# Loading x's first half and the first weight word in small transfers on two queues, in a two-layer encoder on one Trainium2 core

## The chip, the core and the metric

The kernel runs on one core of one Trainium2 chip. Its parts here are TensorE (PE: matrix products and the turning of 128x128 blocks; PEld is its weight load), VectorE (DVE), ScalarE (ACT), GpSimd (POOL) and SyncE (SP). Transfers from memory are issued by SP, ACT and POOL, each with a queue of its own (q1 is SP's, q10 is ACT's), and share 16 DMA engines. The metric is the device time of one execution in microseconds; before the change the median of three runs is 907.72 us (907.42 to 908.06).

## The reference

Two layers over x of 256 tokens by 1024 features, in float32. Each layer is: half a SwiGLU, a mixer (an mLSTM in layer 0, windowed attention in layer 1), half a second SwiGLU, each followed by a layer norm of `ALPHA * x + ...`:

```python
def swiglu(x, w_in, w_out):
    gu = x @ w_in
    g, u = gu[..., :D_FF], gu[..., D_FF:]
    return (jax.nn.silu(g) * u) @ w_out

def reference(x, ...):
    for l in range(DEPTH):
        x = layer_norm(ALPHA * x + 0.5 * swiglu(x, ffn_w_in[l, 0], ffn_w_out[l, 0]), ln_g[l, 0], ln_b[l, 0])
        j = l // N_MIXERS
        if l % N_MIXERS == 0:
            y = mlstm_mixer(x, ml_w_in[j], ml_gate_b[j], ml_norm_g[j], ml_w_out[j])
        else:
            y = window_attention(x, at_w_in[j], at_sink[j], at_w_out[j])
        x = layer_norm(ALPHA * x + y, ln_g[l, 1], ln_b[l, 1])
        x = layer_norm(ALPHA * x + 0.5 * swiglu(x, ffn_w_in[l, 1], ffn_w_out[l, 1]), ln_g[l, 2], ln_b[l, 2])
    return x
```

The change touches only what happens ahead of and during the first products of the first SwiGLU, `x @ w_in`.

## The kernel before

**Products.** Every float32 operand is split in two parts of a shorter format, high (`_hi`) and low (`_lo`), and each product is made of three: high x high, low x high and high x low. For x the split needs x turned: TensorE turns 128x128 blocks of x with the identity matrix `ident` (rows `py<-ident,x`), one engine casts the turned block to `xT_hi` and DVE subtracts to get `xT_lo`. x lies in two tiles of 128 tokens (`x_72`, `x_73` in the instruction lists), each loaded in two halves of 512 features. The products read `xT` as the stationary operand and a word of weights as the moving one.

**Words.** Weights come in words of 128 partitions by 1024 numbers (512 KB). A word lands in `w_raw` (four buffers, and one further one later) or `s_raw` (words that are also summed with others); ACT casts it to `w_hi`, DVE subtracts to get `w_lo`. Only word 0 is cast and subtracted in two halves of 512 numbers (one for each 128 rows of the weight matrix), so that its first products can start after the first half.

**The opening.** ACT issues the four loads of x (tile 0 half 0, tile 1 half 0, tile 0 half 1, tile 1 half 1), then loads its activation table. SP issues the words: as many as there are buffers, then each further one when a buffer comes free. `ident` is made on POOL and DVE. In `ffn`, at the very start, TensorE runs `warm(14)`, 14 idle turns of `ident` into a bank that nobody reads; then turns tile 0's half 0, whose cast is DVE's; then `warm(8)`. The function `first_mm` then writes out the order of the first two words: for word 0 the high x high pair for tile 0, the turns of tile 1's half 0 (cast by ACT), the x-low pair, the w-low pair, and the three pairs for tile 1; for word 1 first the turns of both second halves (eight turns), then the pairs.

**What sets the order elsewhere.** TensorE's order is the program's. The casts, subtractions and sums of words are placed by a planner (`Paced` and `Weights.fill`): it keeps a model of each engine's time and of when each load lands (`moving`, with constants for issuing, landing and loading), and after each product decides which cast, subtraction or sum fits next; a freed buffer then lets SP issue the next word. So a change in the modelled time of the opening can change the order of later words on ACT, DVE and SP. Each engine runs its own list strictly in order.

## Time and profile before

| | |
|---|---|
| median of three runs | 907.72 us (907.42 to 908.06) |
| profiled execution, first to last instruction (span) | 906.0 us |
| around the span (median less span) | 1.7 us |
| TensorE busy | 896.5 us, 4419 products and turns |
| DVE, ACT, POOL busy | 799.4, 568.9, 142.0 us |
| x's first quarter lands | 5.39 us after the span's start |
| first product | 6.93 us |

The page gives the profiled execution's time as its span; the runs' times are 1.7 us above it, and the same is taken for both kernels. How to read the rows quoted below: a timeline row has the start in us, the length in us, engine, line, operation, written tile <- read tiles, shape, count, and in brackets how long the engine had been idle and what ended that. A row of the waits has who waited, for whom, us in total, times, the longest. A row of the windows has the window, its length, the busy time of PE, PEld, DVE, ACT and POOL with instruction counts, the granted TensorE clock, the DMA share and GB/s. A tile's row has an engine, operation and tiles, a count, and the shortest, median and longest length in ns with the first and last start. A queue's row has the packets so far, MB, and the share of the 16 engines. L179 is the line of the helper that records every operation, so rows are told apart by their tiles.

### The profile page before, as it was taken

Reading aid. Unit: us, or ns where it says so; the run is one execution under the profiler, and the core shown is the slowest. Engines: PE = TensorE matmul, PEld = TensorE weight load, DVE = VectorE, ACT = ScalarE, POOL = GpSimd, SP = SyncE. Lnnn points to the kernel's source line nnn. Section 1 sums busy time; section 2 is a strip of 40 time slices with the busy share of each in tenths; the row PEclk is TensorE's granted clock in tenths of the full one; section 3 lists DMA queues with packets and bytes.
Section 4 is the critical chain, followed back from the end, with each engine's and each line's share of the span. In section 5 each row is a group of like instructions: output and inputs, shape, how many; then the busy total and the mean of one; then the engine's idle time right before and its main releaser. Section 6 shows DMA issues by size and latency. Waiting matters only on the chain.

```text
span 906.0 us, 12445 instructions
## 1 busy us (share of the span) xinstructions
PE 896.5 (99%) x4419; PEld 748.8 (83%) x4419; DVE 799.4 (88%) x971; ACT 568.9 (63%) x782; POOL 142.0 (16%) x177
## 2 busy tenths in 40 slices
PE   9999999999999999999999999999999999999996
PEld 7888888889988888888888888888897788888885
DVE  5999899877799898999988899998867899899985
ACT  5776777356664666766636676765568566676760
POOL 0111123112211011211011112110414111111110
PEclk9999999999999999999999999999999999999999
DMA  8999998545637888998868989987333788899851
GB/s 278 367 321 274 256 301 218 171 141 182 214 99 248 306 233 238 290 274 247 235 202 280 241 265 275 286 203 238 122 111 117 246 267 257 207 302 267 243 140 47
DMA packets 100734, 208.54 MB, mean 230 GB/s; under 512 B 6920, under 2 KB 21296, under 8 KB 100672
## 3 DMA queue, kind: packets, MB, share of 16 engines
q1 hardware_dynamic: 82368, 173.04, 54.7%
q0 software_dynamic: 17728, 33.66, 22.1%
q10 hardware_dynamic: 576, 1.05, 0.3%
q8 instruction: 35, 0.57, 0.2%
q14 instruction: 27, 0.22, 0.1%
HBM read 206.65 MB, written 1.05 MB: 229 GB/s over the span
## 4 chain that ended last, share of the span: by engine, by line
PE 98%; DVE 1%; DMA 1%; issue 0%; DVEq 0%
PE pw L179 63%; PE py L179 35%; DMA x<-in_x_dram 1%; DVE x L179 0%; DVE w_lo L179 0%; DVE stats L179 0%; DVE pr L179 0%; DVEq L1622 0%; DVE q_lo L179 0%; DVE mv L179 0%; DVE rs L179 0%
## 5 line engine op out<-in xcount | busy, mean ns | idle before, releaser
L179 DVE TENSOR_TENSOR w_lo<-w_raw,w_hi 128x1024 fp32r<-128x1024 f32 (+1 forms) x213 | 255.0, 1217 | 24.9 <-ACT w_hi L179 23.2
L179 ACT CAST w_hi<-w_raw 128x1024 fp32r<-128x1024 f32 (+1 forms) x213 | 218.8, 1049 | 73.2 <-PE py L179 18.8
L179 DVE TENSOR_TENSOR w_lo<-s_raw,w_hi 128x1024 fp32r<-128x1024 f32 x192 | 228.3, 1217 | 18.0 <-ACT w_hi L179 18.0
L179 ACT CAST w_hi<-s_raw 128x1024 fp32r<-128x1024 f32 x192 | 196.4, 1054 | 59.8 <-DVE s_raw L179 30.4
L179 PE MATMUL pw<-w_hi,xT_hi 128*128 128x512 f32 x480 | 156.1, 395 | 0.0
L179 PE MATMUL pw<-w_hi,xT_lo 128*128 128x512 f32 x480 | 153.5, 390 | 0.0
L179 PE MATMUL pw<-w_lo,xT_hi 128*128 128x512 f32 x480 | 153.4, 390 | 0.0
L120 POOL DMA_DIRECT2D s_raw<-in_ffn_w_in_dram x64 | 77.4, 1210 | 482.6 <-DVE s_raw L179 253.5
L179 PE MATMUL py<-w_hi,h_hi 128*128 128x512 f32 x349 | 117.3, 396 | 0.0
L179 PE MATMUL py<-w_hi,h_lo 128*128 128x512 f32 x349 | 115.5, 390 | 0.0
L179 PEld LDWEIGHTS pw<-w_lo,xT_hi 128*128 128x128 f32 x480 | 90.1, 188 | 19.0 <-DVE w_lo L179 0.3
L179 PEld LDWEIGHTS pw<-w_hi,xT_lo 128*128 128x128 f32 x480 | 90.0, 188 | 19.0
L179 PE MATMUL py<-w_lo,h_hi 128*128 128x512 f32 x349 | 104.8, 390 | 0.0
L179 PEld LDWEIGHTS pw<-w_hi,xT_hi 128*128 128x128 f32 x480 | 88.1, 188 | 16.5 <-ACT w_hi L179 0.2
L179 PE MATMUL pw<-w_hi,S_lo 128*128 128x512 f32 x256 | 78.8, 389 | 0.0
L179 PE MATMUL pw<-w_hi,S_hi 128*128 128x512 f32 x256 | 78.8, 389 | 0.0
L179 PE MATMUL pw<-w_lo,S_hi 128*128 128x512 f32 x256 | 78.8, 389 | 0.0
L179 PEld LDWEIGHTS py<-w_hi,h_lo 128*128 128x128 f32 x349 | 65.5, 188 | 14.4 <-DVE h_lo L179 0.4
L179 DVE TENSOR_TENSOR s_raw<-s_raw,s_raw 128x1024 f32<-128x1024 f32 x64 | 76.7, 1218 | 0.3
L179 PEld LDWEIGHTS py<-w_lo,h_hi 128*128 128x128 f32 x349 | 65.6, 188 | 13.4
L179 PEld LDWEIGHTS py<-w_hi,h_hi 128*128 128x128 f32 x349 | 64.7, 188 | 12.6 <-DVE S L179 0.2
L179 PEld LDWEIGHTS pw<-w_hi,S_lo 128*128 128x128 f32 x256 | 48.1, 188 | 10.0
(201 smaller groups left out, 1084.4 us busy)
## 6 DMA issues: line engine op xcount, KB each, us to landing
s_raw<-in_ffn_w_in_dram SPq DMA_DIRECT2D x96, 512.0 KB, 8.0
w_raw<-in_ffn_w_out_dram SPq DMA_DIRECT2D x88, 512.0 KB, 6.6
w_raw<-in_ffn_w_in_dram SPq DMA_DIRECT2D x64, 512.0 KB, 6.3
s_raw<-in_ffn_w_in_dram POOLq DMA_DIRECT2D x64, 512.0 KB, 8.3
w_raw<-in_ml_w_in_dram SPq DMA_DIRECT2D x24, 512.0 KB, 4.6
w_raw<-in_ffn_w_in_dram SPq DMA_DIRECT2D x32, 256.0 KB, 5.7
w_raw<-in_at_w_in_dram SPq DMA_DIRECT2D x12, 512.0 KB, 4.6
w_raw<-in_ml_w_out_dram SPq DMA_DIRECT2D x8, 512.0 KB, 3.9
```

The source lines that it names most:

```text
L120: self.nc.gpsimd.dma_start(ap, source, accum_op=OP.add)
L179: r = f(out, *args, **kw)
```

## The change

A new function `load_both` issues one load as two, rows 0 to 63 on SP's queue and rows 64 to 127 on ACT's, and tells the planner's model of it once. The two first halves of x (both tiles) go through it in place of one load on ACT's queue each. Word 0 goes through it twice, once for each half of 512 numbers. The second halves of x stay on ACT's queue, every other word on SP's. The idle turns ahead of the first products go from 14 to 10 and from 8 to 6.

```diff
+    def load_both(self, ap, source):
+
+        for r, engine in ((slice(0, 64), self.nc.sync), (slice(64, 128), self.nc.scalar)):
+            engine.dma_start(ap[r], source[r])
+        self.moving(0, ap, LANDING, LOADING * int(np.prod(ap.shape[1:])) / 1024, ISSUING)
+
...
-            nc.load(t.rearrange("p (k f) -> p k f", k=self.words[i]["k"]), self.words[i]["src"])
+            to = t.rearrange("p (k f) -> p k f", k=self.words[i]["k"])
+            if i == 0:
+                for k in range(self.words[i]["k"]):
+                    nc.load_both(to[:, k], self.words[i]["src"][:, k])
+            else:
+                nc.load(to, self.words[i]["src"])
...
-        nc.load(xt[t][:, s_], x[0, t * 128:(t + 1) * 128, s_], nc.nc.scalar)
+        if h == 0:
+            nc.load_both(xt[t][:, s_], x[0, t * 128:(t + 1) * 128, s_])
+        else:
+            nc.load(xt[t][:, s_], x[0, t * 128:(t + 1) * 128, s_], nc.nc.scalar)
...
-                warm(14)
+                warm(10)
                 to_xT(0, xt[0], ybank, (0,), nc.vector.tensor_copy)
                 W.split(1)
-                warm(8)
+                warm(6)
```

ACT, from its first instruction, before (DMA is the issue of a load; `x_72` and `x_73` are the two token tiles, `w_raw` a word):

```order
L111 DMA x_72<-in_x_dram 128x512
L111 DMA x_73<-in_x_dram 128x512
L111 DMA x_72<-in_x_dram 128x512
L111 DMA x_73<-in_x_dram 128x512
L593 ACT_TABLE_LOAD
L179 CAST w_hi<-w_raw 128x512 x2
L179 CAST xT_hi<-py 128x4x128
```

and with the change:

```order
L122 DMA x_72<-in_x_dram 64x512
L122 DMA w_raw<-in_ffn_w_in_dram 64x512 x2
L122 DMA x_73<-in_x_dram 64x512
L111 DMA x_72<-in_x_dram 128x512
L111 DMA x_73<-in_x_dram 128x512
L607 ACT_TABLE_LOAD
L185 CAST w_hi<-w_raw 128x512 x2
L185 CAST xT_hi<-py 128x4x128
```

Six issues stand ahead of the table load and the first cast in place of four, and the second halves of x come fifth and sixth in place of third and fourth.

SP, from its first instruction, before (an `s_raw` is a word that is also summed, `L114` a word in two strips):

```order
L116 DMA w_raw<-in_ffn_w_in_dram 128x2x512 x8
L116 DMA s_raw_211<-in_ffn_w_in_dram 128x2x512
L114 DMA w_raw<-in_ffn_w_in_dram 128x2x256 x2
L116 DMA s_raw_222<-in_ffn_w_in_dram 128x2x512
L114 DMA w_raw<-in_ffn_w_in_dram 128x2x256 x4
L116 DMA s_raw_257<-in_ffn_w_in_dram 128x2x512
```

and with the change:

```order
L122 DMA x_72<-in_x_dram 64x512
L122 DMA w_raw<-in_ffn_w_in_dram 64x512 x2
L122 DMA x_73<-in_x_dram 64x512
L116 DMA w_raw<-in_ffn_w_in_dram 128x2x512 x7
L116 DMA s_raw_210<-in_ffn_w_in_dram 128x2x512
L114 DMA w_raw<-in_ffn_w_in_dram 128x2x256 x2
L116 DMA s_raw_225<-in_ffn_w_in_dram 128x2x512
L114 DMA w_raw<-in_ffn_w_in_dram 128x2x256 x2
L116 DMA s_raw_240<-in_ffn_w_in_dram 128x2x512
```

Word 1 is now SP's fifth issue in place of its second, and further on a summed word goes ahead of a strip word.

DVE, ahead of the third down product (between the first two turns of `hh` of 256 columns and the `h_lo` of 512), before:

```order
L179 TENSOR_TENSOR hh_487<-sg_485,pw_380 128x256
L179 TENSOR_TENSOR w_lo_499<-w_raw_359,w_hi_449 128x1024
L179 TENSOR_TENSOR w_lo_512<-w_raw_387,w_hi_475 128x1024
L179 TENSOR_TENSOR w_lo_523<-s_raw0_211,w_hi_505 128x1024
L179 TENSOR_TENSOR w_lo_534<-s_raw0_257,w_hi_516 128x1024
L179 TENSOR_TENSOR s_raw0_211<-s_raw0_211,s_raw2_361 128x1024
L179 TENSOR_TENSOR s_raw0_257<-s_raw0_257,s_raw2_389 128x1024
L179 TENSOR_TENSOR w_lo_559<-w_raw_423,w_hi_527 128x1024
```

and with the change:

```order
L185 TENSOR_TENSOR hh_484<-sg_482,pw_373 128x256
L185 TENSOR_TENSOR w_lo_496<-w_raw_346,w_hi_448 128x1024
L185 TENSOR_TENSOR s_raw0_210<-s_raw0_210,s_raw2_384 128x1024
L185 TENSOR_TENSOR w_lo_515<-s_raw0_240,w_hi_475 128x1024
L185 TENSOR_TENSOR w_lo_526<-s_raw1_225,w_hi_502 128x1024
L185 TENSOR_TENSOR s_raw0_240<-s_raw0_240,s_raw2_394 128x1024
L185 TENSOR_TENSOR w_lo_543<-w_raw_400,w_hi_519 128x1024
L185 TENSOR_TENSOR w_lo_555<-w_raw_406,w_hi_530 128x1024
```

The word that TensorE uses last ahead of the third down product (`w_lo_499` before, `w_lo_543` with the change) moves from the first place behind `hh` to the sixth. The lists of all engines are the same again from about the place that the trace before reaches at 60 us, and TensorE's list differs only in the two counts of idle turns.

## The prediction

> **What bounds the kernel now.** I read the page's busy times and chain first, then the waits of TensorE.
>
> ```profile
> PE 896.5 (99%) x4419; PEld 748.8 (83%) x4419; DVE 799.4 (88%) x971; ACT 568.9 (63%) x782; POOL 142.0 (16%) x177
> PE 98%; DVE 1%; DMA 1%; issue 0%; DVEq 0%
> PE py L179 <- DVE ident L179: 1.7, 1, 1.7
> PE py L179 <- DMA x<-in_x_dram: 0.4, 1, 0.4
> ```
>
> TensorE (PE) is busy for 896.5 of 906.0 us and carries 98% of the chain. In the whole execution it has two recorded waits, 1.7 us for the identity matrix and 0.4 us for x, both at the start. So the change has only the opening to win. Here are the windows and, merged in order of time, the opening itself (start, length, engine, work):
>
> ```profile
> 0.00:7.00 7.00, 4.85 (x27) 4.25 (x27) 1.10 (x3) 2.42 (x3) 0.47 (x6) 1.00 0.69 236
> 7.00:12.00 5.00, 5.00 (x27) 3.88 (x28) 3.89 (x6) 2.41 (x4) 0.00 (x0) 1.00 1.05 388
> 40.00:60.00 20.00, 20.00 (x92) 16.55 (x91) 20.00 (x21) 13.49 (x17) 3.62 (x3) 1.00 1.07 322
> 0.79 2.54 ACTq L111 DMA_DIRECT2D x<-in_x_dram  x4
> 1.72 3.25 PE L179 MATMUL py<-ident 128*128 128x128 f32 x14 [1.72 <-DVE ident L179]
> 3.37 1.28 ACT L593 ACT_TABLE_LOAD   x1 [3.37 <-issue]
> 5.39 0.66 PE L179 MATMUL py<-ident,x 128*128 128x128 f32 x4 [0.43 <-DMA x<-in_x_dram]
> 5.72 1.14 ACT L179 CAST w_hi<-w_raw 128x512 fp32r<-128x512 f32 x2 [1.07 <-DMA w_raw<-in_ffn_w_in_dram]
> 6.09 0.69 DVE L179 CAST xT_hi<-py 128x512 fp32r<-128x512 f32 x1 [4.43 <-PE py L179]
> 6.82 0.69 DVE L179 TENSOR_TENSOR xT_lo<-py,xT_hi 128x512 fp32r<-128x512 f32 x1
> 6.93 0.70 PE L179 MATMUL pw<-w_hi,xT_hi 128*128 128x512 f32 x2
> 7.42 1.28 DVE L179 TENSOR_TENSOR w_lo<-w_raw,w_hi 128x512 fp32r<-128x512 f32 x2
> 7.50 0.42 PEld L179 LDWEIGHTS py<-ident,x 128*128 128x128 f32 x4 [0.31 <-DMA x<-in_x_dram]
> 7.92 0.70 PE L179 MATMUL pw<-w_hi,xT_lo 128*128 128x512 f32 x2
> 8.20 0.59 ACT L179 CAST xT_hi<-py 128x512 fp32r<-128x512 f32 x1 [1.34 <-PE py L179]
> 8.46 0.80 PE L179 MATMUL pw<-w_lo,xT_hi 128*128 128x512 f32 x2
> 8.76 0.19 PEld L179 LDWEIGHTS pw<-w_lo,xT_hi 128*128 128x128 f32 x1 [0.34 <-DVE w_lo L179]
> 9.10 0.62 PE L179 MATMUL pw<-w_hi,xT_hi 128*128 128x512 f32 x2
> 9.56 0.63 PE L179 MATMUL pw<-w_lo,xT_hi 128*128 128x512 f32 x2
> 10.48 1.03 PE L179 MATMUL py<-ident,x 128*128 128x128 f32 x8
> 11.27 0.71 PE L179 MATMUL pw<-w_hi,xT_hi 128*128 128x512 f32 x2
> ```
>
> The reader is to see two branches that meet at 6.93. In one, x's first quarter lands (5.39), is turned by TensorE, and is cast by DVE (6.09 to 6.78). In the other, the first word of weights lands and ACT casts its halves from 5.72 to 6.86. Behind 6.93 a pair of products starts 0.46 us after the one before (9.10, 9.56), four turns take 0.41 (7.51 to 7.92) and eight 0.79 (10.48 to 11.27). From 6.93 to 11.27 lie six pairs, four turns and eight: 6 x 0.46 + 0.41 + 0.79 = 3.96 of 4.34 us. The other 0.38 us is short waits, mostly for x (7.50) and for w_lo (8.76). Behind 11.27 TensorE waits for nothing in either window, so what is gained or lost by then passes to the end unchanged. I use 11.27, the first pair behind the eight turns, as the mark.
>
> **The change, part by part.** Durations of the issues, and how many packets each queue had moved by 3.5 us (first two queue rows) and 4.5 us:
>
> ```profile
> L111 ACTq DMA_DIRECT2D x<-in_x_dram x4: 453/489/1027, 0.8 to 2.3; - x4
> DMA to landing us min/median/max: 4.6/6.8/8.2
> q1 hardware_dynamic: 82, 0.17, 28.4%
> q10 hardware_dynamic: 32, 0.07, 4.9%
> q1 hardware_dynamic: 194, 0.40, 35.3%
> q10 hardware_dynamic: 127, 0.25, 14.2%
> ```
>
> *x's first quarter* (q10 is ACT's queue). It is 128 packets of 2 KB; 127 packets of q10 had started by 4.5 and the landing was seen at 5.39, so landing follows by 0.9 us. By 3.5 us both queues together had started 114 packets, but most of them were weights. With x at the head of both queues its 128 packets are out between 3.6 (all share evenly) and 3.85 (ACT's queue, the slower one, needs 64: between its 32 at 3.5 and 127 at 4.5). Plus 0.9 that is 4.5 to 4.75; I take 4.65, 0.74 earlier. The turns, DVE's cast (0.70 behind the turns' start, as 5.39 to 6.09) and the product (0.15 behind the cast's end of 6.78) move along: the x branch allows the first product at 6.93 - 0.74 = 6.2.
>
> *The first word.* Its first half is packets 129 to 256, and 321 had started by 4.5: about 4.25 + 0.9 = 5.15. But ACT now issues six transfers before its table load, not four. Three of the four took some 0.48 us, the last 1.03. The next two cost 0.45 to 1.03 each, and if the long one goes with larger transfers, all six may take 0.45. So the table load starts between 0.79 + 6 x 0.46 = 3.6 and 0.79 + 3 x 0.48 + 3 x 1.03 = 5.3, and ends 1.28 later, at 4.9 to 6.6. I take one long issue and five short: 0.79 + 5 x 0.48 + 1.03 = 4.2, end 5.5. Casts then run 5.55 to 6.69 in place of 5.72 to 6.86: the word's branch gains only 0.17. Cover that hid four issues (they ended at 3.33, the word came at 5.72) is used up by six.
>
> *The sum.* First product 6.2; the second needs the second cast half, 6.69 + 0.07 = 6.76. The turns of x's second row block follow at 6.76 + 0.23 = 6.99 (its data is behind 512 packets, about 5.4 + 0.9 = 6.3, so the wait at 7.50 is gone). Then come xT_lo's pair at 7.40 and w_lo's at 7.86; DVE, 0.74 earlier than at 7.42 to 8.70, makes w_lo from 6.68 to 7.96, in time for both products. The next pair needs ACT's cast of the turned block, 0.69 + 0.59 behind the turns' start, as 7.51 to 8.20 to 8.79: 8.27, so 8.35. It and two more pairs end at 9.73, the eight turns at 10.52: the mark comes 0.75 earlier. The last x block now leaves ACT behind five other transfers. It landed at 2.3 + 8.2 = 10.5, and its turns want it at 9.73 + 0.4 = 10.13. If it lands as before, the mark is 10.5 + 0.41 = 10.91, a gain of 0.36. With half of x's first blocks moved to SP's queue it should come somewhat earlier. Between 0.36 and 0.75 I take **0.6 us**.
>
> *Idle turns.* Eight of 22 go. They cost nothing where they wait for x anyway; the first ten end well before 4.65. What they cover is the clock:
>
> ```profile
> L179 PE MATMUL py<-ident x14: 421/421/476, 1.7 to 4.5; 128*128 128x128 f32 x14
> L179 PE MATMUL py<-ident x8: 272/272/273, 5.9 to 6.7; 128*128 128x128 f32 x8
> ```
>
> The first 14 take 421 ns each and start 0.215 us apart, the later ones 272 ns. So TensorE was at a lower speed until after 4.5 and at full speed by 5.39, though the windows' clock column shows 1.00 throughout. Ten turns end near 4.0, and a gap of 0.6 us follows. This could delay the step; it is a rival below, and costs nothing in the forecast.
>
> The Trainium skill ("TensorE: Matmul & The Clock Gate", section "The HAM clock gate (the "warmup" mystery)") says that the clock doubles after a free-running window of about 3.4 us of sustained work. The trace agrees in kind: 3.25 us of turns, then the faster ones. By that rule a window with ten turns and a gap in it may not count, which speaks against this edit; an estimate from the page's 3.4 us puts the step at 4.65 + 3.4 = 8.05 then, where the rows give 7.9 (rival 1).
>
> *The order behind it.* The planner now takes other words first, on ACT, DVE and SP, up to about 60 us; TensorE's order stays. From 40 to 60 us DVE is busy 20.00 of 20.00, so a word pushed back there could come late. The one pushed back most is the second weight word ahead of the third down product (w_lo_499 before, w_lo_543 now).
>
> ```profile
> 43.43 2.35 DVE L179 TENSOR_TENSOR w_lo<-w_raw,w_hi 128x1024 fp32r<-128x1024 f32 x2
> 53.15 0.61 PE L179 MATMUL pw<-w_lo,xT_hi 128*128 128x512 f32 x2
> ```
>
> It was started at 43.43 and used at 53.15. Five steps of its length (2.35 / 2 = 1.18 us) now stand ahead of it: start 49.3, ready 50.5. TensorE wants it 2.6 us later, 2.0 us if TensorE is 0.6 early and DVE is not. I cost this at nothing.
>
> **Rivals.** 1. *The clock comes later (slower).* It decides if the step to full speed waits for another unbroken 3.25 us of work. From the restart at 4.65 that is 7.9. Until then turns start 0.215 apart and pairs, at the same ratio, some 0.9. Four turns 4.65 to 5.5, six idle ones to 6.8, the first pair to 7.7, four turns to 8.2 (one slow, three fast), five pairs to 10.5, eight turns: the mark at 11.3, no change, **907.7**. So 7.9 is the point from which it decides: each us that the step comes later costs 0.5. If a stretch is broken again, the next ends at 11.15; halfway, 9.5, costs 0.8: **908.5**, and 11.15 costs 1.6: 909.3. For it: ten turns and a gap. Against it: only 0.6 us is missing, and turns of x fill in.
>
> 2. *The table load is late.* At its upper bound the casts run 6.6 to 7.74, the second product at 7.81, 1.05 behind the forecast's: 0.6 becomes -0.4, **908.1**; halfway, no change. For it: the fourth issue's 1.03 us. Against: half as many rows in each transfer.
>
> 3. *The transfers do not do what they are for.* Smaller ones start no sooner: q1 and q10 moved 114 packets by 3.5 us, whoever owned them. With x at 5.2 only 0.2 is won: **907.5**.
>
> 4. *A word comes late* at 50 to 53 us, if DVE slips by over 2.0 us, say because one of the sums ahead of it has to wait for its transfer. A slip of 3 us would cost 1.0 and leave **908.1**. For it: DVE is full there. Against: TensorE's two recorded waits are both at the start, so such margins have held everywhere.
>
> **Numbers.** The median is 907.72, 1.7 us above the profiled span of 906.0; I take that rest as fixed. Forecast: 907.72 - 0.6 = **907.1**, chance 0.53 (own range 906.7 to 907.5). Clock 0.17 (half of it beyond 7.9), table load 0.15, no earlier landing 0.10, late word 0.05. With the upper bound of the gain (casts at 5.2, from the word's landing: first two products unbroken, 0.33 more and about 1.0 in all, 906.7), the slower rivals at 908.1 to 908.5 and some 0.3 of scatter below (the runs shown span 0.64), I give 906.3 to 908.5. A measurement of this kernel can tell about 0.2%, 1.8 us. The gain cannot reach that: with x at 4.5 at the earliest and 1.54 from its landing to the first product (5.39 to 6.93) it is 0.9 there, and 0.38 of waits behind it, 1.3 in all. Only a clock that misses its second stretch, or a late word on top of another loss, comes near it on the other side. So faster 0.04, same 0.91, slower 0.05.
>
> **What would show it.** The first turns of x at 4.65 (right if 4.4 to 4.9); ACT's table load starting at 4.2 and the first cast at 5.55; the pair behind the eight turns at 10.5 to 10.9 in place of 11.27; the turns of x 272 ns long at once, where 421 would mean rival 1; and no new wait of TensorE between 12 and 60 us. The prediction is wrong if that mark does not move, or if the span changes by more than the mark.

## The result: 2.1 us slower, and the profile after

The changed kernel takes **910.17 us** in the median of ten runs (908.83 to 913.10) against 908.10 us for ten runs of the kernel before beside them: ratio 1.0028, 95% interval 1.0020 to 1.0036. A second measurement (further down) gives 1.0039, 1.0026 to 1.0053. The forecast was 907.1 us, in a range of 906.3 to 908.5, with a chance of 0.05 for slower. It was wrong in sign. Two of the runs further down, one of 1093 us (word 0 in whole rows) and one of 1295 us (first quarter only), had a granted clock of 0.78 and 0.65 in place of 0.99 or more and are left out of every comparison.

The profiled execution has a span of 908.2 us against 906.0. From the page of the changed kernel, busy time:

```profile
PE 898.0 (99%) x4413; PEld 750.0 (83%) x4413; DVE 799.7 (88%) x971; ACT 568.3 (63%) x782; POOL 142.1 (16%) x177
```

TensorE is busy 1.5 us longer with six turns fewer (4413 in place of 4419 instructions): it has not more to do, it does it more slowly. The opening of the changed kernel, in order of time (L185 is the helper, before it was L179; columns as in the prediction's rows):

```profile
0.80 0.57 ACTq L122 DMA_DIRECT2D x<-in_x_dram  x1
1.40 1.26 ACTq L122 DMA_DIRECT2D w_raw<-in_ffn_w_in_dram  x2
2.68 0.62 ACTq L122 DMA_DIRECT2D x<-in_x_dram  x1
3.55 1.45 ACTq L111 DMA_DIRECT2D x<-in_x_dram  x2
...
4.21 1.09 PE L185 MATMUL py<-ident,x 128*128 128x128 f32 x4
5.03 1.28 ACT L607 ACT_TABLE_LOAD   x1 [5.03 <-DMA w_raw<-in_ffn_w_in_dram]
5.08 1.49 PE L185 MATMUL py<-ident 128*128 128x128 f32 x6
6.32 1.14 ACT L185 CAST w_hi<-w_raw 128x512 fp32r<-128x512 f32 x2
6.99 1.31 PE L185 MATMUL pw<-w_hi,xT_hi 128*128 128x512 f32 x2 [0.42 <-ACT w_hi L185]
8.30 1.08 PE L185 MATMUL py<-ident,x 128*128 128x128 f32 x4
9.04 1.20 PE L185 MATMUL pw<-w_hi,xT_lo 128*128 128x512 f32 x2
10.04 0.96 PE L185 MATMUL pw<-w_lo,xT_hi 128*128 128x512 f32 x2
10.83 0.62 PE L185 MATMUL pw<-w_hi,xT_hi 128*128 128x512 f32 x2
12.21 1.03 PE L185 MATMUL py<-ident,x 128*128 128x128 f32 x8
13.01 0.70 PE L185 MATMUL pw<-w_hi,xT_hi 128*128 128x512 f32 x2
```

The first turns of x start at 4.21, earlier than forecast. But the first product is at 6.99 (before 6.93), and the mark, the pair behind the eight turns, is at 13.01 in place of 11.27: 1.74 us later. The first product waits for the first cast, and in this profile the cast waits for ACT's table load, which ends at 6.31. The word's first half was there before. The first row gives the landings of its two loads (issued at 1.40 and 1.44), the second those of x's second block (issued at 2.68 and 2.98):

```profile
DMA to landing us min/median/max: 3.2/3.7/4.1
DMA to landing us min/median/max: 4.9/5.1/5.2
```

So the word's first half had landed by 5.5, and x's second block landed at 8.2. Three things are new, then: the first product is held by the table load; the turns of x's second block start at 8.30 in place of 7.51; and everything up to the pair at 10.04 runs slowly (four turns 1.08 and 1.09 us, a pair 1.31 and 1.20), as the rows of the turns, for the first 12 us, show:

```profile
L185 PE MATMUL py<-ident x16: 417/417/473, 1.7 to 6.2; 128*128 128x128 f32 x16
L185 PE MATMUL py<-ident,x x8: 417/421/446, 4.2 to 9.0; 128*128 128x128 f32 x8
```

No turn up to 9.0 us takes the 272 ns that the eight idle turns took before; TensorE reaches full speed only ahead of the pair at 10.83 (0.62 long). The 1.74 us split so: the second block late, 8.30 less 7.51 = 0.79; its turns 0.74 us up to the next pair in place of 0.41, +0.33; that pair 1.00 up to the next in place of 0.54, +0.46; the next 0.79 in place of 0.64, +0.15; from there both kernels take the same (2.18 and 2.17). So 0.94 is the slow clock. The 0.79 has two causes that overlap: the block landed at 8.2, and the slow pair ahead of it would by itself have held the turns until about 8.0 (an estimate: its second product starts at 7.58, and later slow products follow each other by 0.43).

TensorE's waits in the whole execution:

```profile
PE py L185 <- DVE ident L185: 1.7, 1, 1.7
PE pw L185 <- ACT w_hi L185: 0.4, 1, 0.4
PE py L185 <- DVE S L185: 0.3, 1, 0.3
```

The wait for x is gone from the list and one for w_hi has come: the word's cast now comes last. (The wait ahead of 8.30 does not appear: the row before it is drawn up to 8.30, and the idle time of the weight load is put down to "issue".) The third wait, at 503 us, adds some 0.4 us to the shift; it is treated with the run on the order.

What the queues moved between 3 and 8 us, before and then after (the last column is GB/s):

```profile
3.00:8.00 5.00, 4.57 (x29) 3.65 (x27) 1.88 (x3) 2.42 (x3) 0.00 (x0) 1.00 1.01 383
```

```profile
3.00:8.00 5.00, 4.48 (x18) 3.27 (x16) 2.41 (x4) 2.42 (x3) 0.00 (x0) 1.00 0.91 234
```

The DMA engines are nearly as busy (0.91 against 1.01) and deliver 234 in place of 383 GB/s. The prediction counted packets at the pace of the kernel before. Up to 5.5 us that pace held (524 packets of both queues against 537), but 98 of them were small ones under 512 B in place of 32. From 5.5 to 8 us only 296 packets started in place of 532.

### The profile page after: what moved, and what is told of

It is laid out like the page before. It is cut to its first block, busy times and chain, and to the rows that moved or that the text cites. A ratio compares the mean times of both kernels' runs of the same rounds, so it can differ in the third digit from the quotient of the medians.

```text
span 908.2 us, 12436 instructions
## 1 busy us (share of the span) xinstructions
PE 898.0 (99%) x4413; PEld 750.0 (83%) x4413; DVE 799.7 (88%) x971; ACT 568.3 (63%) x782; POOL 142.1 (16%) x177
## 3 DMA queue, kind: packets, MB, share of 16 engines
q10 hardware_dynamic: 608, 1.05, 0.4%
HBM read 206.65 MB, written 1.05 MB: 229 GB/s over the span
## 4 chain that ended last, share of the span: by engine, by line
PE 95%; DVE 2%; DMA 1%; ACT 0%; issue 0%; ACTq 0%; DVEq 0%
PE pw L185 60%; PE py L185 35%; DMA w_raw<-in_ffn_w_out_dram 1%; DVE w_lo L185 1%; DMA w_raw<-in_ffn_w_in_dram 0%; DVE x L185 0%; DVE s_raw L185 0%; DVE S L185 0%; ACT w_hi L185 0%; DVE stats L185 0%; DVE S_lo L185 0%; ACT L607 0%; DVE pr L185 0%; DVEq L1636 0%; DVE q_lo L185 0%
## 5 line engine op out<-in xcount | busy, mean ns | idle before, releaser
L185 DVE TENSOR_TENSOR w_lo<-w_raw,w_hi 128x1024 fp32r<-128x1024 f32 (+1 forms) x213 | 255.1, 1219 | 26.4 <-ACT w_hi L185 25.2
L185 ACT CAST w_hi<-w_raw 128x1024 fp32r<-128x1024 f32 (+1 forms) x213 | 218.4, 1050 | 70.9 <-PE py L185 20.9
L185 DVE TENSOR_TENSOR w_lo<-s_raw,w_hi 128x1024 fp32r<-128x1024 f32 x192 | 228.6, 1219 | 17.9 <-ACT w_hi L185 17.8
L185 ACT CAST w_hi<-s_raw 128x1024 fp32r<-128x1024 f32 x192 | 196.5, 1054 | 61.0 <-DVE s_raw L185 31.7
L185 PE MATMUL pw<-w_hi,xT_hi 128*128 128x512 f32 x480 | 156.6, 397 | 0.4 <-ACT w_hi L185 0.4
L185 PE MATMUL pw<-w_hi,xT_lo 128*128 128x512 f32 x480 | 154.0, 391 | 0.0
L185 PE MATMUL pw<-w_lo,xT_hi 128*128 128x512 f32 x480 | 153.6, 391 | 0.0
L185 PE MATMUL py<-w_hi,h_hi 128*128 128x512 f32 x349 | 117.5, 396 | 0.3 <-DVE S L185 0.3
L185 PE MATMUL py<-w_hi,h_lo 128*128 128x512 f32 x349 | 115.3, 390 | 0.0
L185 PEld LDWEIGHTS pw<-w_hi,xT_lo 128*128 128x128 f32 x480 | 90.3, 188 | 19.0
L185 PEld LDWEIGHTS pw<-w_lo,xT_hi 128*128 128x128 f32 x480 | 90.4, 188 | 18.8
L185 PE MATMUL py<-w_lo,h_hi 128*128 128x512 f32 x349 | 104.9, 390 | 0.0
L185 PEld LDWEIGHTS pw<-w_hi,xT_hi 128*128 128x128 f32 x480 | 88.5, 189 | 17.5 <-ACT w_hi L185 1.1
L185 PE MATMUL pw<-w_lo,S_hi 128*128 128x512 f32 x256 | 78.8, 389 | 0.0
L185 PE MATMUL pw<-w_hi,S_hi 128*128 128x512 f32 x256 | 78.8, 389 | 0.0
L185 PE MATMUL pw<-w_hi,S_lo 128*128 128x512 f32 x256 | 78.8, 389 | 0.0
L185 PEld LDWEIGHTS py<-w_hi,h_lo 128*128 128x128 f32 x349 | 65.5, 188 | 14.1 <-DVE h_lo L185 0.2
L185 DVE TENSOR_TENSOR s_raw<-s_raw,s_raw 128x1024 f32<-128x1024 f32 x64 | 76.8, 1219 | 0.3
L185 PEld LDWEIGHTS py<-w_lo,h_hi 128*128 128x128 f32 x349 | 65.6, 188 | 13.4
L185 PEld LDWEIGHTS py<-w_hi,h_hi 128*128 128x128 f32 x349 | 64.6, 188 | 13.2 <-DVE S L185 0.7
L185 PEld LDWEIGHTS pw<-w_hi,S_hi 128*128 128x128 f32 x256 | 48.0, 188 | 10.0
```

What stands on the lines that cost most here:

```text
L185: r = f(out, *args, **kw)
```

## The experiments

Sixteen kernels ran, in four sets (one of them before again, one the change again), each beside runs of the kernel before on the same chip (their medians: 907.52, 907.44, 907.37 and 907.21 us). The differences below are medians against those; intervals are of the ratio.

### Loads and turns apart

The change with the idle turns put back, the turns alone, and each of the two split loads alone:

```diff
 # turns back: the change, with
-                warm(10)
+                warm(14)
-                warm(6)
+                warm(8)
 # turns only: before, with the same lines the other way round
 # x only: turns back, and word 0 whole
-            if i == 0:
+            if i < 0:
 # word only: turns back, and x whole
-        if h == 0:
+        if h < 0:
```

> The change with its idle turns put back to 14 and 8; the loads stay split. In the changed kernel TensorE's turns were 417 ns long up to 9.0 us and the pair behind the eight turns came at 13.01 in place of 11.27. Theory 'clock': the fewer idle turns let the step to full speed slip from before 5.4 us to after 10 us, and that is most of the loss. Then the turns of x's second block are 272 ns long, the mark comes at 11.3 to 11.8 (the first cast at 6.3 and the second block's landing at 8.2 stay late), and the time is 0.0 to 0.5 us above the kernel before. Theory 'loads': eight small issues of 0.6 us each delay ACT's table load and the second block of x, and that is the loss whatever the clock does. Then the mark stays at 12.5 or later and the time 1.3 us or more above the kernel before.

> The kernel before with only the idle turns cut to 10 and 6; every load and every engine's order as before. Theory 'clock': the step to full speed slips here too, since TensorE now stands still from about 4.1 to 5.4 us: turns of 417 ns beyond 5.4, and 1 to 2.5 us above the kernel before. Theory 'loads': no change, within 0.2 us, since the turns cut were only waiting.

> Only x's first halves are split over both queues; word 0 is one load on SP's queue as before, and the idle turns are 14 and 8. ACT has four issues ahead of its table load, as before. Theory 'clock': no loss, and at most 0.4 us gained, as the first product waits for word 0, which now stands behind a half of x on SP's queue (landing at about 6.0 in place of 5.7). Theory 'loads': the loss comes from the small issues of word 0, so none here; a time 0.3 us above to 0.4 us below the kernel before by this one too. It tells how much of the split is harmless: over 1 us above would put the loss on x's split itself.

> Only word 0 is split in four small loads on both queues; x is loaded as before, the idle turns are 14 and 8, and the order of the words on ACT, DVE and SP up to 60 us is that of the change. Theory 'clock': within 0.5 us of the kernel before. Theory 'loads': ACT's table load starts at about 4.5 to 5.0, the first cast near 6.3, x's second block lands after 8, and the time is 1 us or more above the kernel before. A theory 'order' (the planner's other order of the words costs something near 500 us, where the changed kernel's profile lost 0.4 us) expects the same 0.4 here and in the run with the turns put back.

| | median, us | against before | ratio | mark in the profile |
|---|---|---|---|---|
| turns back | 908.78 | +1.26 | 1.0016 (1.0007 to 1.0024) | 11.90 |
| turns only | 908.30 | +0.78 | 1.0006 (0.9998 to 1.0015) | 10.91 |
| x only | 911.53 | +4.01 | 1.0041 (1.0027 to 1.0055) | 14.74 |
| word only | 910.06 | +2.54 | 1.0031 (1.0019 to 1.0044) | 13.46 |

Loads alone and turns alone give 1.26 + 0.78 = 2.04, close to the 2.07 us of the first measurement; the second gives 3.90, so that the sum fits may be chance. A mark is that of one execution: the one of turns only is among its fastest (907.23), the one of word only above its median (911.25). The turns' part is a tendency only: its interval holds 1, its fastest runs (907.23) are as fast as before's and others reach 909.3. With the turns back, the opening reads:

```profile
4.76 0.91 PE L185 MATMUL py<-ident,x 128*128 128x128 f32 x4
5.36 1.28 ACT L607 ACT_TABLE_LOAD   x1 [5.36 <-DMA w_raw<-in_ffn_w_in_dram]
7.33 1.02 PE L185 MATMUL pw<-w_hi,xT_hi 128*128 128x512 f32 x2 [0.78 <-ACT w_hi L185]
8.25 0.63 PE L185 MATMUL py<-ident,x 128*128 128x128 f32 x4
```

Here the clock steps up during the first turns of x. What is left is the late first product (7.33), whose cast waits for the table load up to 6.64 (the word's first half had landed by 5.1), and the late second block (landed at 8.1, turned at 8.25). The early x brings nothing either: 14 turns end at 4.76. Splitting x alone is worse than splitting both. The row of its first cast says why:

```profile
8.20 1.14 ACT L185 CAST w_hi<-w_raw 128x512 fp32r<-128x512 f32 x2 [3.76 <-DMA w_raw<-in_ffn_w_in_dram]
8.87 1.32 PE L185 MATMUL pw<-w_hi,xT_hi 128*128 128x512 f32 x2 [2.16 <-ACT w_hi L185]
```

Word 0, whole and second on SP's queue, lands at 8.2 in place of 5.72. TensorE idles 2.16 us, and the pair behind that takes 1.32 us: behind the idle stretch the clock goes down again, until about 12.5. So a late landing cost twice here.

### Is it ACT's table load?

In the changed kernel's instruction list two of ACT's loads wait for earlier ones to complete (eight counters serve the loads of both queues, and eight half loads take them all), and the table load stands behind them:

```
L111 DMA x_72<-in_x_dram 128x512 [waits DMAHW0_49]
L111 DMA x_73<-in_x_dram 128x512 [waits DMAHW2_49]
L607 ACT_TABLE_LOAD
```

The edit, on the kernel with the turns back, moves the table load ahead of these two.

```diff
+    nc.scalar.preload_act_table(AF.Silu)
...
-    nc.scalar.preload_act_table(AF.Silu)
```

> The change with 14 and 8 idle turns, and ACT's table load issued ahead of x's two second halves. With the table load behind them it started at 5.36 (its queue waited for earlier loads to land before it could issue the sixth, up to 5.0), and the first cast at 6.66. Theory 'table': that wait is what the split loads cost. Then the table load starts at 3.3, the first cast at about 5.5, and the time falls by 0.8 us or more against the change with 14 and 8 turns (1.26 above the kernel before), to within 0.4 of the kernel before. Theory 'late second block': x's second block landed at 8.2 in place of 7.5, since each small load follows the one ahead of it on its queue by 1.1 to 2 us whatever its size. Then the first product moves to about 6.3, TensorE waits for x at 8.2, and the time stays 0.8 us or more above the kernel before.

909.84 us, +2.4 (ratio 1.0027, 1.0016 to 1.0037): not better than with the turns back.

```profile
3.33 1.28 ACT L604 ACT_TABLE_LOAD   x1 [3.33 <-issue]
6.64 1.14 ACT L185 CAST w_hi<-w_raw 128x512 fp32r<-128x512 f32 x2 [2.03 <-DMA w_raw<-in_ffn_w_in_dram]
8.74 0.63 PE L185 MATMUL py<-ident,x 128*128 128x128 f32 x4 [0.40 <-DMA x<-in_x_dram]
```

The table is there at 4.61 and ACT then waits 2.03 us for the word itself, which lands at 6.64. The table load alone is not the cause: with it out of the way the word is late by itself, the second block comes later still (8.74), and the time does not fall. But where it stands behind the two waiting loads, the table load does set the first cast. It ends at 6.31 in the change, at 6.64 with the turns back and at 6.84 in the change measured again, and in all three the word's first half had landed by 5.1 to 5.5.

### Word 0 in whole rows, one split quarter, and more turns

```diff
 # word 0 as two loads of 128 whole rows, both on SP's queue: before, with
+            if i == 0:
+                nc.nc.sync.dma_start(to[:, 0], self.words[i]["src"][:, 0])
+                nc.nc.sync.dma_start(to[:, 1], self.words[i]["src"][:, 1])
 # first quarter only: before, and in load_x
+        if h == t == 0:
+            nc.load_both(xt[t][:, s_], x[0, t * 128:(t + 1) * 128, s_])
 # more turns: before, with
-                warm(14)
+                warm(18)
-                warm(8)
+                warm(10)
```

> The kernel before, with word 0 as two loads of 256 KB one behind the other on SP's queue in place of one of 512 KB; x, ACT's list, the idle turns and every other order as before. Theory 'a load follows its forerunner by over 1 us whatever its size': the first half lands no earlier than the whole word did (5.3 to 5.7), the second about 1 us later, and the time is 0.3 to 1.0 us above the kernel before. Theory 'table' expects no loss, as ACT's list is unchanged: within 0.2, or 0.2 less if the first half lands early.

> The kernel before, with only x's first quarter split over both queues; word 0 then stands second on SP's queue, behind 64 rows of x, and ACT issues four loads ahead of its table load as before. Theory 'a load follows its forerunner': x's first quarter lands near 4.2, but word 0 lands 0.7 to 1.5 us later than at 5.7, the first product comes at 7.6 or later, and the time is 0.6 to 1.5 us above the kernel before. Theory 'table': ACT has as many issues as before, so no loss, and a gain of up to 0.4 from x.

> The kernel before with 18 and 10 idle turns in place of 14 and 8 (10 and 6 cost 0.8 us in the median, with the fastest runs unchanged). Theory 'clock': the turns decide how often the step to full speed comes in time; with more of them the slow half of the runs (907.5 to 909.1) moves to the fast half, and the median falls by 0.1 to 0.3 us, or the four turns' own 0.2 to 0.4 us eat that. If the turns were only waiting time, 18 turns at 0.215 us end at 5.6 and push x's turns by 0.2 to 0.5 us: the median and the fastest runs both rise by that.

Word 0 in two loads of whole rows: 908.19 us, ratio 1.0007 (0.9998 to 1.0016). Its first half lands at 4.88, the mark is at 11.02, and the rate stays up:

```profile
3.00:8.00 5.00, 4.76 (x30) 4.03 (x29) 2.15 (x4) 2.39 (x4) 0.00 (x0) 1.00 1.00 378
```

So cutting a load in two is not shown to cost by itself. One quarter of x by rows is enough for a loss: 908.62 us, ratio 1.0029 (1.0015 to 1.0043; it follows the mean more than the median), in two groups, seven runs at 908.1 to 908.8 and four at 912.5 to 913.6. The profiled execution is of the second group:

```profile
4.60 0.60 PE L185 MATMUL py<-ident,x 128*128 128x128 f32 x4
9.63 1.14 ACT L185 CAST w_hi<-w_raw 128x512 fp32r<-128x512 f32 x2 [5.36 <-DMA w_raw<-in_ffn_w_in_dram]
10.30 1.02 PE L185 MATMUL pw<-w_hi,xT_hi 128*128 128x512 f32 x2 [4.22 <-ACT w_hi L185]
12.76 1.05 PE L185 MATMUL pw<-w_lo,xT_hi 128*128 128x512 f32 x2
```

x is early, word 0 lands at 9.63, TensorE idles 4.22 us, and soon behind that it is slow until about 14.5 (a pair at 12.76 still takes 1.05). More turns: 908.06 us, ratio 1.0005 (0.9996 to 1.0013), in a narrow band (907.25 to 908.29). They push the turns of x to 5.61. Neither fewer nor more turns than fourteen and eight can be told from no change.

### Half the partitions, many loads, or few rows?

```diff
 # alternate rows: turns back, and in load_both
-        for r, engine in ((slice(0, 64), self.nc.sync), (slice(64, 128), self.nc.scalar)):
+        for r, engine in ((slice(0, 128, 2), self.nc.sync), (slice(1, 128, 2), self.nc.scalar)):
 # columns: turns back, and in load_both
+        for r, engine in ((slice(0, 256), self.nc.sync), (slice(256, 512), self.nc.scalar)):
+            engine.dma_start(ap[:, r], source[:, r])
 # word by halves: before, with
+                nc.nc.sync.dma_start(to[:, 0], self.words[i]["src"][:, 0])
+                nc.nc.scalar.dma_start(to[:, 1], self.words[i]["src"][:, 1])
```

> The change's loads with the idle turns of before (14 and 8), as in the run with the turns put back, but the two halves of each split load are the even and the odd rows in place of rows 0 to 63 and 64 to 127. Count of loads, their size (128 KB), their pieces (2 KB) and both queues stay. Theory 'half of the partitions': a load that writes 64 neighbouring partitions moves slowly (190 to 260 GB/s between 3 and 8 us against 350 to 405 for whole loads), so here the rate is back at 340 or more, both halves of word 0's first half have landed by 5.0 to 5.6, x's second block by 7.0, the mark is at 11.3 or earlier and the time within 0.5 us of before. Theory 'many small loads': the rate stays at 190 to 260, word 0 and x's second block land at 5.3 and 8.2 again and the time is about 1.3 us above before.

> As the run before it, but the two halves are by columns: 128 rows of 256 numbers on each queue, so pieces are 1 KB in place of 2 KB and their number doubles. Theory 'half of the partitions': all 128 partitions are written by each load, so the rate is above 260 GB/s unless small pieces cost by themselves; time within 0.8 us of before. Theory 'many small loads': as with the split by rows, 190 to 260 GB/s and 1.3 us or more above before. A rate back for alternate rows but not here would say that the size of a piece counts as well.

> The kernel before with one edit: word 0 as two loads of 128 whole rows by 512 numbers (256 KB), the first half on SP's queue and the second on ACT's behind its first instruction; loads of x and idle turns as before. If whole rows keep the rate (350 GB/s and more from 3 us), word 0's first half lands 0.5 to 1 us earlier than in before (under 5.2) but x's quarter is not earlier, or later by up to 0.7 us where the second half of the word is ahead of it on ACT's queue; the first product is at 6.5 to 7.6 and the time between 0.5 below and 0.7 above before. If the split alone cost, whatever its shape, it would be 1 us or more above before.

> The kernel before unchanged, measured as if it were a change: ratio 1.000 with an interval of about 0.001 to each side. Its profile, taken on the same chip as the others, shows how much the landings scatter from one execution to the next with identical loads: x's first quarter between 4.4 and 5.4, the mark between 10.9 and 11.5. If the ratio is off by more than 0.0006, differences of that size between the other kernels are not to be read.

The kernel before, as a control, has ratio 1.0003 (0.9994 to 1.0012): differences of 0.0003 say nothing. Its profile, with a span of 905.3, shows how far one execution is from the next with the same loads:

```profile
4.75 1.06 PE L179 MATMUL py<-ident,x 128*128 128x128 f32 x4
5.37 1.14 ACT L179 CAST w_hi<-w_raw 128x512 fp32r<-128x512 f32 x2 [1.11 <-DMA w_raw<-in_ffn_w_in_dram]
5.61 1.57 PE L179 MATMUL py<-ident 128*128 128x128 f32 x8
6.93 0.71 PE L179 MATMUL pw<-w_hi,xT_hi 128*128 128x512 f32 x2
11.04 0.70 PE L179 MATMUL pw<-w_hi,xT_hi 128*128 128x512 f32 x2
```

x has landed by 4.4 (issued at 0.79, 3.6 us to landing), not at 5.39, and TensorE turns it straight behind the fourteen idle turns; so the wait of 0.4 us for x, from which the prediction drew its gain, is not there in every execution. And the clock is still low in the idle turns from 5.61 on (eight take 1.57 us), though in the first profile it had stepped by 5.39.

Alternate rows: 911.00 us, ratio 1.0042 (1.0029 to 1.0055). Columns: 908.75, ratio 1.0016 (1.0007 to 1.0025). The rates, of alternate rows and then of columns:

```profile
3.00:8.00 5.00, 4.66 (x24) 4.18 (x22) 2.03 (x4) 2.52 (x3) 0.00 (x0) 1.00 0.86 250
```

```profile
3.00:8.00 5.00, 4.15 (x25) 3.53 (x24) 2.35 (x4) 2.42 (x3) 0.00 (x0) 1.00 0.99 310
```

The theory of half the partitions fell: alternate rows reach over all of them and are as slow (250 GB/s) as neighbouring ones (261 with the turns back). The count of loads alone does not do it either: columns have the same count and size, in pieces half as long, and move at 310.

The landings say it more sharply. x's second block landed at 8.1 with the turns back and at 9.75 with alternate rows, but at 6.2 by columns (the control: 6.4). By 5.5 us the columns had moved 1.07 MB, the kernel before 1.03 and the change 0.87. What the columns lose stands elsewhere in their opening:

```profile
5.09 1.28 ACT L607 ACT_TABLE_LOAD   x1 [5.09 <-DMA w_raw<-in_ffn_w_in_dram]
11.65 0.63 PE L185 MATMUL py<-ident,x 128*128 128x128 f32 x4 [0.37 <-DMA x<-in_x_dram]
```

The word's first half had landed by 4.7, but its cast waits for the table load up to 6.37; and the last x block, issued only at 4.7, holds TensorE up at 11.65. Both stand behind the loads that wait for a completion. So in this profile those waits cost by themselves, even with landings in time. The loss of the columns is as large as that of neighbouring rows with the turns back (ratio 1.0016 each); how much of the rows' loss is the late block and how much the held-up issues is therefore not separated.

Here a rule of the Trainium skill stands against the change, and I had not weighed it. "SBUF — State Buffer", section "Can I just issue two DMAs to hit both halves?", says that two transfers at once, one from partition 0 and one from partition 64, gave only 6% over one, and that all ports are reached only by one transfer over all partitions. The trace agrees that two halves by rows do not add up to a whole (234 against 383 GB/s). Its reason, the ports that a transfer's partitions reach, does not explain the alternate rows, which by the same page's formula for ports would reach every one: the measured 250 decides.

Word 0 by halves on two queues: 909.22 us, ratio 1.0021 (1.0012 to 1.0030), at the full rate (387 GB/s between 3 and 8 us). The word's second half, behind x's first quarter on ACT's queue, is cast at 6.83 and delays x's second block to 8.30; the mark is at 11.91. So even at the full rate, sharing out the order of the two queues anew moved the lateness elsewhere.

### Rows on one queue, fewer columns, and the order alone

What was open: whether the 64 rows or the two queues make the loads slow, what the waits for counters cost, and the planner's order.

```diff
 # rows on one queue: before, with
+        if (t, h) == (0, 0):
+            for r in (slice(0, 64), slice(64, 128)):
+                nc.nc.scalar.dma_start(xt[t][r, s_], x[0, t * 128:(t + 1) * 128, s_][r])
 # few columns: before, with load_both by columns for x's first quarter, and
+                nc.load_both(to[:, 0], self.words[i]["src"][:, 0])
+                nc.load(to[:, 1], self.words[i]["src"][:, 1])
 # order alone: before, word 0 in one load, the planner's model told of it in two halves
+                for k in range(self.words[i]["k"]):
+                    nc.moving(0, to[:, k], LANDING, LOADING * 512 / 1024, ISSUING)
```

> The kernel before with one edit: x's first quarter as two loads of 64 rows, both on ACT's queue (in the run with only that quarter split, one was on each queue). Theory 'loads of 64 rows': the rate from 3 to 6 us is low again (200 to 260 GB/s where before has 334 to 401), something behind lands late, and the time is 0.8 us or more above before. Theory 'a load shared by two queues': rate 330 or more, x's quarter and word 0 land as in before within 0.5 us, and the time is within 0.5 us of before.

> Idle turns 14 and 8. Only x's first quarter and the first half of word 0 are split, by columns (128 rows by 256 numbers on each queue); the rest goes in whole rows, so that eight loads are out before one has to wait for a completion counter. Theory 'counters make the dip': no slice from 4 to 9 us below 340 GB/s, word 0's first half lands by 5.0 and x's second block by 7.0, the mark is at 10.6 to 11.2 and the time within 0.4 us of before. Theory 'many loads cost whatever waits for them': rate 237 to 300 in some slice again and 0.8 us or more above before.

> The kernel before with the planner's model told of word 0 as the change tells it (two halves): loads and idle turns as before, but the casts, subtractions, sums and later loads in the change's order. My step 'the order costs nothing' expects a ratio within 0.0005 of 1 and the pairs from 20 us on within 0.1 us of before's, beside the shift of the opening. If the order costs, TensorE has a new wait between 20 and 60 us or near 500 us, and the time is 0.4 us or more above before.

> The change unchanged, beside the same runs of before as the three others: 2.1 us above before (1.5 to 2.8). The profile should show the late landings again (word 0 at 5.5 to 6.6, x's second block at 7.6 to 8.2 or later) and turns of x of 421 ns at first; where the clock steps can differ by some us from the first profile, and the mark with it by half of that.

**Rows on one queue**: 911.67 us, +4.5 (ratio 1.0051, 1.0037 to 1.0066). Packets by 5.5 us, of before and then of this kernel, and its opening:

```profile
q1 hardware_dynamic: 366, 0.72, 44.1%
q10 hardware_dynamic: 171, 0.32, 15.1%
```

```profile
q1 hardware_dynamic: 428, 0.84, 57.6%
q10 hardware_dynamic: 80, 0.13, 6.8%
```

```profile
5.26 1.14 ACT L179 CAST w_hi<-w_raw 128x512 fp32r<-128x512 f32 x2
8.13 0.63 PE L179 MATMUL py<-ident,x 128*128 128x128 f32 x4 [3.17 <-DMA x<-in_x_dram]
8.60 1.76 PE L179 MATMUL py<-ident 128*128 128x128 f32 x8
```

Same queue, same bytes, same place; only that 128 rows go as 64 and 64. ACT's queue then moves 80 packets in the time of 171, while SP's whole words take the share that is left, and x is turned at 8.13 in place of 5.39. The first 64 rows alone land at 5.7, later than all 128 did before (5.4), the second 64 at 8.0. The two queues are not needed for the loss: **here the loads of 64 rows moved slowly and yielded to the whole loads beside them**. In the run with only the first quarter split it was otherwise: both halves landed by 4.2, the whole word behind one of them on SP's queue came late (9.63), and the whole load of x behind the other on ACT's queue came early (4.8, before 7.5). So a queue with a load of 64 rows in it can fall behind the other queue; what decides which one does is open. The rate did not fall to the 200 to 260 that this theory expected (321 GB/s from 3 to 8 us, since SP's words fill in), so its number was off; the landing decides. Why 64 rows are slow is not settled: the partitions reached are not it (alternate rows), and the trace does not name the DMA engine of a packet.

**Few columns**: 907.83 us, +0.6 (ratio 1.0010, 1.0001 to 1.0020). Between the two theories: the mark is at 11.04, as in the control, and x's second block is turned without a wait, but the rate still dips. It is 331 GB/s from 3 to 8 us; the slices from 5 to 7 us had 305 and 307, below the 340 that the theory of the counters allowed. With half the split loads the loss is about half (columns in all four: 310 GB/s, +1.4), though the two intervals overlap. Whether counters or shorter pieces make the dip is not settled; that all four by columns moved 1.07 MB by 5.5 us speaks against the pieces. It is no improvement on before.

**Order alone**: 907.74 us, ratio 1.0005 (0.9996 to 1.0014). The casts, subtractions and sums stand exactly in the change's order. TensorE has no wait between 12 and 60 us. The wait for `S` at 503 us appears here (0.2 us), but as well in the word by halves, which has before's order (0.2 us), and not in the control or in the few columns, which has the change's. It comes and goes with small shifts of the loads in a stretch where DVE is full; the order is not shown to cost anything that a measurement here can tell.

**The change again**: 911.11 us, +3.9 (ratio 1.0039, 1.0026 to 1.0053), above the 1.5 to 2.8 us expected. In this profile:

```profile
6.85 1.14 ACT L185 CAST w_hi<-w_raw 128x512 fp32r<-128x512 f32 x2
7.52 1.02 PE L185 MATMUL pw<-w_hi,xT_hi 128*128 128x512 f32 x2 [0.99 <-ACT w_hi L185]
9.22 0.63 PE L185 MATMUL py<-ident,x 128*128 128x128 f32 x4 [0.67 <-DMA x<-in_x_dram]
12.08 1.05 PE L185 MATMUL pw<-w_lo,xT_hi 128*128 128x512 f32 x2
```

The first cast (6.85, again straight behind the table load) and the second block (9.22) are later still, and a pair at 12.08 is slow. The mark is at 14.36. In these profiles, how much the change costs depends on the execution: how late the loads are, and how long the clock stays down behind them.

## Why the prediction was wrong, step by step

**"At the head of both queues its 128 packets are out between 3.6 and 3.85 ... I take 4.65."** The mechanism was right and the landing better than said: the first turns of x start at 4.21, ahead of its bounds of 4.4 to 4.9. It earned nothing, since the word's cast came last.

**"Its first half is packets 129 to 256 ... about 4.25 + 0.9 = 5.15", and x's second block "behind 512 packets, about 5.4 + 0.9 = 6.3".** The second figure is the step that failed first. The block landed at 8.2, in the change measured again at 9.1, with the turns put back at 8.1. The prediction took split loads to land at the pace of whole ones. Packets started as fast as before up to 5.5 us, but a part of them were small ones that its count left out, and then the pace fell: 234 to 261 GB/s from 3 to 8 us in place of 383. That the late landing goes with the rows, and not with the count of loads, the run by columns shows (6.2), though it lost as much time by held-up issues; that two queues are not needed, the run with 64 rows on one queue. The word's first half was nearly right where the table load stood behind other loads (5.1 to 5.5), and late where it did not (6.64). The forecast's gain of 0.6 on the mark became 0.6 of loss by the loads alone, the table load among them (turns put back: 11.90 against 11.27, one execution each).

**The table load at 4.2.** It came at 5.03 and ended at 6.31, inside the bounds of 4.9 to 6.6. So the first cast, forecast for 5.55, came at 6.32. The cause was not in the sum, which priced six issues but no wait between them: ACT's fifth and sixth loads wait for the completion of earlier ones, and the last is through at 5.00. Rival 2, a late table load, has the right sign and the right place. It is not the whole: with the table loaded early the time stayed, since the word and the block were then late by themselves.

**"Idle turns ... costs nothing in the forecast."** Failed in this profile. (Six of the 22 turns go, not the eight that the prediction counts.) In the profile the clock steps after the pair at 10.04, and 0.94 of the 1.74 us are slow turns and products. Rival 1, the later clock, had about the right price: each us past 7.9 costs 0.5, so a step at about 10.6 costs 1.35 and puts its mark of 11.3 at 12.65; it was at 13.01. What it may have lacked is that late landings feed it. The x-only and first-quarter runs show that idle stretches of 2.2 and 4.2 us bring the clock down without any turn being removed; and with ten and six turns but whole loads the turns of x at 7.35 were already fast (four in 0.60 us). That the short stretches of the change (0.42 us ahead of 6.99, and up to 8.30) kept it down is argued and not shown. Taken alone, ten and six turns cost +0.78 us, not distinguishable from nothing.

The Trainium skill ("TensorE: Matmul & The Clock Gate", section "The HAM clock gate (the "warmup" mystery)") calls the window free-running, so that the step varies from run to run. The control agrees: with the same fourteen turns the step lay behind 5.61 us, in the first profile ahead of 5.39.

**"The order ... at nothing."** Held within what can be told: 1.0005, with an interval around 1.

**The last x block, the bound on 0.36.** It did not decide here: the eight turns ran unbroken from 12.21.

**The rest of 1.7 us and "behind 11.27 what is gained or lost passes to the end unchanged".** Nearly right: 1.74 at the mark and 2.2 in the span; the wait at 503 us added 0.4. The rest outside the span held: the profiled run took 909.97, 1.8 us above its span of 908.2.

**The range.** Its bounds came from single rivals. The unknown cost, the landing of a load of 64 rows, was not in it at all: the rows of before show only whole loads, and "half as many rows in each transfer" was even put down as a point for an early table load. Then two rivals, the table load and the clock, came together with late landings of the second block, for which there was no rival.

## What to carry to other kernels

Before splitting a load into fewer rows than 128, look at a trace of such halves: here they lost the rate, while columns landed in time and blocks of whole rows kept the rate. No split here was faster than the whole load. Price a split by the landing of a load of that shape, not by the packets per us of another shape. Count the loads in flight too: in this kernel the ninth waits for an earlier one, and holds up what stands behind it on its engine. Where a stall is 0.4 us in one profile, look at a second execution before building on it: here x's landing moved by 1.0 us (5.4 and 4.4) and the clock's step by more than 1 us with nothing changed. And a late landing near the start can be paid twice, once as the wait and once as the slow clock behind it.

## What was not expected of the hardware

- With all four loads split into 64 rows, neighbouring or alternate, on two queues: 234 to 261 GB/s between 3 and 8 us at a DMA share of 0.85 to 0.95; with only some of them split, 277 to 299. With no load of fewer than 128 whole rows: 360 to 387. On one queue beside whole words: 80 packets by 5.5 us in place of 171.
- Issuing ACT's four half loads took 0.57 to 0.62 us each in the change, and 0.45 to 0.49 for three of the four whole loads of before (the fourth 1.03); by columns 0.42 to 0.45. It is not the load's own shape alone: with 64 rows on one queue, the three whole loads of x behind them took 0.61 to 0.62.
- One split quarter of x gave two groups of times, 908.1 to 908.8 and 912.5 to 913.6 us, 4 us apart, with the same program.
- TensorE's clock fell again behind an idle stretch of 2.2 us and came back 3 to 4 us after work resumed (x only: resumed at 8.87, the first weight load still at full speed with 0.19 us, the next at 0.29, full again at 12.5).
